# Forty-seven DMA issues moved from the sync engine's queue to GpSimd's in a hybrid attention and mLSTM step

## The chip, the cores and the metric

The kernel runs on one core of one Trainium2 chip. The metric is the device time of one execution in microseconds (us). The core has five engines that work side by side: TensorE (PE, matrix products), VectorE (DVE), ScalarE (ACT), GpSimd (POOL) and the sync engine (SP). Each works through its own list of instructions in order. DMAs are issued by an engine's queue: an issue waits in its place in that list until its semaphores allow it, and whatever stands behind it on the same engine waits too. Nearly all DMAs of this kernel are issued by SP, a few by ACT, and two by POOL.

## The reference, cut to what matters

One layer of a diffusion backbone on 128 context tokens and 1024 latent tokens (nine blocks of 128), with rows of 1024 numbers:

```python
h = rmsnorm(x, norm1_w) * (1 + sc1) + sh1
aq, ak, av, mq, mk, mv, mo, mg = jnp.split(h @ w_in, SPLIT_POINTS, axis=-1)
...
attn_o = attention(aq, keys, vals)          # 8 query heads, 2 key heads
...
hm = (hm.reshape(B, T, MLSTM_WIDTH) * jax.nn.sigmoid(mo.astype(F32))).astype(x.dtype)
mix = jnp.concatenate([attn_o, hm], axis=-1) @ w_out
x = x + g1 * mix
h2 = rmsnorm(x, norm2_w) * (1 + sc2) + sh2
x = x + g2 * swiglu(h2, w_gu, w_down)
```

`hm` is the result of a bidirectional mLSTM (a matrix memory, scanned in chunks of 128 tokens). The shifts, scales and the gates `g1` and `g2` come from the conditioning, one set for context tokens and one for latent tokens. The outputs are the normalised rows `y`, the new keys and values, and the mLSTM states.

## The kernel before, in words

The nine blocks of tokens are taken in three groups of three (block 0 holds the context tokens). The input projection and the mLSTM heads come first; beside the projections of the four heads the attention of the three groups is woven in (lines 1740 to 1748). Group 0 keeps its attention results in SBUF. The results of groups 1 and 2 are stored to DRAM, block by block, as `o_d` (line 1164); the last of group 2 are made while the FFN of group 0 already runs.

At the end of the mLSTM stage POOL makes the weighted values `wv` for the memory update (line 840), multiplies and normalises the results (lines 970 and 977) and the results go to DRAM as `hm_d` (line 982; for the last two blocks of the last head by POOL's own queue).

`prefill` (line 1258) then does the half of the output projection that reads the mLSTM results, block by block, and adds it to the rows with the gate `g1`. The rows of groups 0 and 1 stay in SBUF; those of group 2 (`c == 2`) are loaded, added to by POOL (line 1314) and stored to DRAM as `x1_d` (line 1315). They come back later through `new_x1(2)` (line 1183).

The FFN of group 0 follows in five groups of hidden features (`GROUPS`). `gate_up` (line 1477) loads two weight pieces for each block of 128 features, splits each on ACT and DVE into a high and a low half (`load_piece`, lines 173 to 178), and forms three products for one of full precision. POOL makes the low half of the hidden features (`hl`, line 1497). `down` (line 1500) loads the gate rows `gl` and `gx` for 512 columns (`gate_bc`, lines 1189 and 1193), one buffer each, loads the pieces of `w_down`, and adds each block's product to the rows (`add_gated`, lines 1204 and 1205 on DVE). Raw weights land in two buffers (`raw`); a buffer is free when DVE has made the low half from it (line 145).

Beside it, `attention_side` runs the rest of the attention and the attention half of the output projection for groups 1 and 2 (`attn_out`, line 1406): a pair of gate rows `hmr` (`row_pair`, line 1243), the stored results `o` (line 1416), their halves (line 1418), the products and the gated add. After that the rows are normalised (`stats`, `features6`, line 1554) and transposed by PE (line 124) into operands `Bt` (line 1569) for groups 1 and 2, whose FFN is done together by a seven-product scheme after Strassen (`pair6`, lines 1620 to 1622, and `down6`, lines 1688 to 1690) until the end. `gs6` (line 1853) is one more pair of gate rows.

What sets the order: `hot(n)` raises the priority of a block, `tc.issue_after` puts an instruction behind another one, and `weave` interleaves main and side work by hand. The order on each engine's list is otherwise chosen by a planner that works with estimated times (`TC_OPTS = dict(schedule_with_timeline_sim=True)`, line 1868), and all semaphores are set by it. `dma` is `nc.sync.dma_start` and `pool` is `nc.gpsimd` (lines 55 and 56).

## Time and profile before

| | |
|---|---|
| median of 3 runs | 1530.39 us (1525.09 to 1530.83) |
| the profiled execution | 1527.74 us, its span 1526.0 us |
| PE busy | 1427.3 us (94%) |
| DVE busy | 1129.1 us (74%) |
| ACT busy | 813.6 us (53%) |
| POOL busy | 218.4 us (14%) |
| granted PE clock, mean | 0.979 |
| SP's and ACT's DMA queues | 45.8% and 1.1% of the DMA engines' time |
| POOL's DMA queue | 0.1%, 0.39 MB |

A profile describes one execution. Busy time counts an engine's instructions, not its waits. A line of waits names the engine that waited, what it was about to do, and the instruction or DMA that came last before it could go on; then the total, the number of waits and the longest. A line of DMA issues gives the transfer, the queue (SPq, ACTq, POOLq), the number, the size and, where it can be told, the median time from issue to landing. A line of one source line gives the shortest, median and longest duration in ns. `L1189` is line 1189 of the kernel; lines of a helper such as `sub` (145) or `transpose` (124) stand for many callers, which the names of the tiles tell apart.

### The profile page before, as it was taken

How to read it: one execution, taken by the hardware profiler on the slowest of the kernel's cores; microseconds unless marked ns; L12 is line 12 of the kernel's file. 1: busy time of each engine (PE TensorE's matmuls, PEld its weight loads, DVE VectorE, ACT ScalarE, POOL GpSimd, SP SyncE). 2: the span in 40 equal slices, each digit the busy share in tenths (PEclk: the TensorE clock that was granted, in tenths of full speed). 3: DMA queues.
4: the chain of work that ended last, by engine and by line, in shares of the span. 5: the costliest groups of instructions: out<-in, count | busy, mean ns of one | idle time of the engine just before them, and what ended most of it. 6: DMA issues, size and time to landing. Idle time of an engine off the chain costs nothing. (4 is left out here: it accounts for less than half of the span.)

```text
span 1526.0 us, 22787 instructions
## 1 busy us (share of the span) xinstructions
PE 1427.3 (94%) x8282; PEld 1064.8 (70%) x8282; DVE 1129.1 (74%) x2280; ACT 813.6 (53%) x1525; POOL 218.4 (14%) x310
## 2 busy tenths in 40 slices
PE   6889999998899889999999988989999999999994
PEld 3635667766677667978998977966766667676763
DVE  4978556775867878658678766969877696986857
ACT  5855467956767546555675944735233150523233
POOL 0122423232224335210100100100000000000000
PEclk9999999999999899999999999999999999999997
DMA  9575224553668764768687745334122130412112
GB/s 374 155 222 180 79 70 76 127 109 59 103 146 174 180 207 112 202 173 216 177 194 175 172 128 159 104 117 166 56 83 84 41 125 1 139 49 76 35 35 83
DMA packets 254182, 197.02 MB, mean 129 GB/s; under 512 B 166830, under 2 KB 208006, under 8 KB 254070
## 3 DMA queue, kind: packets, MB, share of 16 engines
q1 hardware_dynamic: 251070, 189.56, 45.8%
q10 hardware_dynamic: 2872, 5.62, 1.1%
q8 instruction: 65, 1.06, 0.3%
q14 instruction: 47, 0.39, 0.1%
q0 software_dynamic: 128, 0.39, 0.1%
HBM read 143.94 MB, written 13.26 MB: 103 GB/s over the span
## 5 line engine op out<-in xcount | busy, mean ns | idle before, releaser
L1621 PE MATMUL mm<-Bt,A 128*128 128x384 f16 x616 | 200.8, 326 | 0.0
L1620 PE MATMUL mm<-Bt,A 128*128 128x384 f16 x616 | 199.4, 326 | 0.5 <-DVE c L1641 0.5
L1622 PE MATMUL mm<-Bt,A 128*128 128x384 f16 x616 | 197.5, 326 | 0.0
L174 ACT CAST whi<-raw 128x1024 fp32r<-128x1024 f32 (+1 forms) x102 | 103.0, 1013 | 134.2 <-DMA raw<-in_w_down_dram 43.9
L145 DVE TENSOR_TENSOR wlo<-raw,whi 128x1024 fp32r<-128x1024 f32 (+1 forms) x102 | 121.3, 1190 | 52.9 <-ACT whi L174 50.5
L1136 DVE SCALAR_TENSOR_TENSOR pl<-pr,st,ph 128x1152 f16<-128x1152 f32 (+1 forms) x72 | 95.2, 1322 | 40.8 <-ACT ph L1135 40.8
L1473 PE MATMUL mm<-aTh,whi 128*128 128x384 f32 x352 | 121.3, 345 | 2.4 <-DVE tn L1492 1.2
L1474 PE MATMUL mm<-aTl,whi 128*128 128x384 f32 x352 | 120.2, 342 | 0.0
L1475 PE MATMUL mm<-aTh,wlo 128*128 128x384 f32 x352 | 120.0, 341 | 0.0
L1132 ACT ACTIVATE pr<-S,st 128x1152 f32<-128x1152 f32 (+1 forms) x72 | 81.5, 1132 | 51.8 <-DVE st L1131 50.5
L1131 DVE TENSOR_REDUCE st<-S 128x1 f32<-128x1152 f32 (+1 forms) x72 | 88.9, 1234 | 21.5 <-PE S L1129 21.4
L526 PE MATMUL wi<-headw,hT 128*128 128x384 f16 x288 | 93.9, 326 | 1.2 <-ACT th L816 1.2
L527 PE MATMUL wi<-headw,hT 128*128 128x384 f16 x288 | 93.9, 326 | 0.0
L528 PE MATMUL wi<-headw,hT 128*128 128x384 f16 x288 | 93.9, 326 | 0.0
L1135 ACT ACTIVATE ph<-pr,st 128x1152 f16<-128x1152 f32 (+1 forms) x72 | 83.7, 1163 | 17.1 <-DVE st L1134 8.5
L1129 PE MATMUL S<-kst,qT 128*128 128x384 f32 (+1 forms) x400 | 86.7, 350 | 3.6 <-ACT pr L1132 3.6
L1620 PEld LDWEIGHTS <-A 128*128 128x128 f16 x616 | 60.2, 98 | 42.5 <-issue 3.5
L1622 PEld LDWEIGHTS <-A 128*128 128x128 f16 x616 | 60.3, 98 | 39.8
L1621 PEld LDWEIGHTS <-A 128*128 128x128 f16 x616 | 60.3, 98 | 39.6 <-issue 0.6
L1606 ACT ACTIVATE A<-S,six 128x1024 f16<-128x1024 f32 x44 | 49.9, 1145 | 71.0 <-PE mm L1622 54.0
L1204 DVE TENSOR_TENSOR t<-mm,hmr 128x512 f32<-128x512 f32 x84 | 54.3, 683 | 41.0 <-PE mm L1690 33.3
L145 POOL TENSOR_TENSOR hl<-tn,hl 128x384 fp32r<-128x384 f32 x22 | 29.8, 1355 | 335.5 <-ACT hl L1496 307.9
(460 smaller groups left out, 3737.8 us busy)
## 6 DMA issues: line engine op xcount, KB each, us to landing
raw<-in_w_gu_dram SPq DMA_DIRECT2D x88, 512.0 KB, 3.4
raw<-in_w_down_dram SPq DMA_DIRECT2D x40, 512.0 KB, 3.8
a<-in_w_ada_dram SPq DMA_DIRECT2D x24, 512.0 KB, 5.6
iraw<-in_w_in_dram SPq DMA_DIRECT2D x32, 256.0 KB, 3.4
x<-in_x_sample_dram SPq DMA_DIRECT2D x11, 512.0 KB, 6.0
raw<-in_w_out_dram SPq DMA_DIRECT2D x10, 512.0 KB
aw<-in_w_ada_dram SPq DMA_DIRECT2D x8, 512.0 KB, 5.3
aw<-in_w_ada_dram SPq DMA_DIRECT2D x16, 256.0 KB, 7.8
```

Of the source, the lines that this page charges most:

```text
L145: (dve if eng == "dve" else pool).tensor_tensor(out=out, in0=full, in1=hi, op=ALU.subtract)
L174: nc.scalar.copy(hi[:, :n], raw[:, :n])
L526: mm(ps[:, :n], ah, wh[:, k % 2, c0 : c0 + n], start=(k == 0), stop=False)
L527: mm(ps[:, :n], ah, wl[:, k % 2, c0 : c0 + n], start=False, stop=False)
L528: mm(ps[:, :n], al, wh[:, k % 2, c0 : c0 + n], start=False, stop=(k == KD - 1))
L1136: dve.scalar_tensor_tensor(out=plv, in0=prv, scalar=st[:, 3:4], in1=phv, op0=ALU.mult, op1=ALU.subtract)
L1473: mm(ps, wh[:, k, :], th[:, k, :], start=(k == 0), stop=False)
L1474: mm(ps, wh[:, k, :], tl[:, k, :], start=False, stop=False)
L1475: mm(ps, wl[:, k, :], th[:, k, :], start=False, stop=(k == KD - 1))
L1620: mm(ps, wh[:, k], bt[:, 0, k], start=first and k == 0, stop=False, skip_group_check=True)
L1621: mm(ps, wh[:, k], bt[:, 1, k], start=False, stop=False, skip_group_check=True)
L1622: mm(ps, wl[:, k], bt[:, 0, k], start=False, stop=k == 3, skip_group_check=True)
```

## The change

Each of these DMAs is issued by POOL instead of SP; nothing else differs in the program text. The issues are the stores of attention results of groups 1 and 2 (line 1164), the loads of group 2's rows (1183), the gate rows of the FFN of group 0 (1189 and 1193), the pairs of gate rows (1243), the stores of group 2's rows in `prefill` (1315), and the loads of the stored attention results (1416).

```diff
@@ attention
-                                dma(spill[i].rearrange("p (k x) -> p k x", k=4), oT[i])
+                                pool.dma_start(spill[i].rearrange("p (k x) -> p k x", k=4), oT[i])
@@ new_x1
-            dma(x1[i], x1_d[i])
+            pool.dma_start(x1[i], x1_d[i])
@@ gate_bc
-        dma(gl, g_d[idx, 1:2, cs].to_broadcast([P, 512]))
+        pool.dma_start(gl, g_d[idx, 1:2, cs].to_broadcast([P, 512]))
...
-        dma(gx, g_d[idx, 0:1, cs].to_broadcast([P, 512]))
+        pool.dma_start(gx, g_d[idx, 0:1, cs].to_broadcast([P, 512]))
@@ row_pair
-            dma(gl, row[n * 512 : (n + 1) * 512].rearrange("(o n) -> o n", o=1).to_broadcast([P, 512]))
+            pool.dma_start(gl, row[n * 512 : (n + 1) * 512].rearrange("(o n) -> o n", o=1).to_broadcast([P, 512]))
@@ prefill, half
-                dma(x1_d[i][:, cs], xt)
+                pool.dma_start(x1_d[i][:, cs], xt)
@@ attn_out
-                dma(o, spilled[i].rearrange("p (k x) -> p k x", k=4))
+                pool.dma_start(o, spilled[i].rearrange("p (k x) -> p k x", k=4))
```

## The prediction

> **What bounds the kernel now.** I read the page first, then busy time by stretches, the waits of TensorE (PE), the waits of the sync engine's queue (SPq), the list of DMA issues, and the timeline where PE stands still. The change touches only work between 422 us, where the first moved store begins to wait, and about 1010 us, where the last gate row is loaded (rows for both stand further down).

> ```profile
> span 1526.0 us, 22787 instructions
> ```
> ```profile
> core 0: us, PE busy (x) PEld busy (x) DVE busy (x) ACT busy (x) POOL busy (x), PEclk, DMA share, GB/s
> 420.00:592.00 172.00, 155.65 (x956) 119.01 (x954) 135.92 (x333) 109.41 (x258) 64.93 (x90) 0.96 0.71 172
> 500.00:592.00 92.00, 79.09 (x451) 60.26 (x450) 77.56 (x211) 51.37 (x112) 35.31 (x34) 0.94 0.67 183
> 592.00:1010.00 418.00, 399.79 (x2160) 359.15 (x2159) 299.10 (x459) 248.63 (x368) 50.31 (x37) 0.99 0.61 163
> 700.00:880.00 180.00, 180.00 (x1038) 165.62 (x1037) 136.43 (x195) 127.38 (x185) 13.81 (x11) 1.00 0.75 186
> ```

> From 592 to 1010 us PE is busy 399.79 of 418 us: 18.2 us are idle, which is all that a better queue could win there. From 700 to 880 us, where most of the moved gate rows fall, nothing is idle. The stretch with more idle time, 500 to 592 us (12.9 us), has one moved DMA issue near it (an attention store at 493 us) and none inside. So PE sets the end of this part, and the first question is whether the 18.2 us come from SP's queue. They are mostly two pauses:

> ```profile
> PE mm L124 <- ACT t L1554: 5.1, 1, 5.1
> PE mm L1215 <- ACT whi L174: 2.8, 1, 2.8
> ```
> ```profile
> 947.23 0.16 DVE L141 SCALAR_TENSOR_TENSOR ry<-rt,ry 128x3 f32<-128x3 f32 x1
> ```
> ```profile
> 949.43 1.88 PE L124 MATMUL mm<-ident,t 128*128 128x128 f32 x8 [5.14 <-ACT t L1554]
> ```

> The longest, 5.1 us, ends at 949.4 us with the transposes of the third group's normalised rows. ScalarE (ACT) makes those rows with the reciprocal root that VectorE (DVE) finishes only at 947.4 us (947.23 + 0.16). A weight that arrived earlier would not have ended this pause. Only the 2.8 us name a weight piece, and the remaining pauses are shorter. Now what SP's queue itself waits for from 592 to 1010 us:

> ```profile
> SPq L173 <- DVE wlo L145: 128.0, 48, 10.1
> ...
> SPq L1193 <- DVE t L1204: 14.4, 5, 5.8
> SPq L1164 <- DVE oS L1158: 11.0, 4, 6.1
> SPq L1189 <- DVE t L1204: 11.0, 6, 3.2
> ```

> The weight loads (line 173) wait 128 us in 48 waits for DVE to give back the raw buffer that they load into, as there are two. The moved DMAs (gate rows at lines 1189 and 1193, attention stores at 1164) hold the queue some 36 us. That looks like much, but a weight load that comes to the head of the queue earlier will in most cases stand there and wait for its buffer.

> **The change part by part.** The moved issues, with their number:

> ```profile
> gl<-g_d SPq DMA_DIRECT2D x12, 256.0 KB
> gx<-g_d SPq DMA_DIRECT2D x10, 256.0 KB, 3.9
> ...
> hm_d<-hm SPq DMA_DIRECT2D x10, 192.0 KB, 5.0
> ...
> o_d<-oS SPq DMA_DIRECT2D x6, 256.0 KB
> ...
> hmr<-g_d SPq DMA_DIRECT2D x6, 256.0 KB
> x_d<-t SPq DMA_DIRECT2D x6, 256.0 KB
> t<-o_d SPq DMA_DIRECT2D x6, 256.0 KB, 3.3
> x<-x_d SPq DMA_DIRECT2D x3, 512.0 KB, 4.3
> ...
> hm_d<-hm POOLq DMA_DIRECT2D x2, 192.0 KB, 2.3
> ```
> ```profile
> L1189 SPq DMA_DIRECT2D gl<-g_d x10: 319/327/835, 638.1 to 1008.3; - x10
> ```
> ```profile
> L982 POOL DMA_DIRECT2D hm_d<-hm x2: 584/650/715, 541.0 to 564.1; - x2
> ```

> Ten of the twelve gl loads move (line 1189; the two of line 1235 stay), with 10 gx, 6 o_d stores, 6 hmr, 6 x_d stores, 6 o_d loads and 3 x_d loads: 47 issues. Bytes and DMA engines stay as they are.

> What SP loses: 47 issues at the median 0.327 us of line 1189, 15.4 us, and the waits ahead of them. What that is worth to PE lies between 0 and all 18.2 idle us. I take 0, because the row nearest to it is the weight loads' 128 us of waiting for buffers, and because the longest pause ends with a DVE chain.

> What POOL gains: 47 issues at 0.65 us (the median of its two own DMAs), 30.6 us. POOL is idle 418 - 50.31 = 367.7 us from 592 to 1010 us, so as work it is hidden. As POOL works in order, each issue also waits there for what it waits for on SP, and what is queued behind it waits too. In the FFN part these are the low halves of the hidden features:

> ```profile
> L145 POOL TENSOR_TENSOR hl<-tn,hl x22: 1005/1023/3711, 648.4 to 1000.1; 128x384 fp32r<-128x384 f32 x22
> ```

> They are 22 in 352 us, and a gate row is waited for while a down projection ends, when the halves of the next group are still to come. So the cover is POOL's idle time, and I cost this at 0. If the cover were gone, one store or load could be held up as one of those halves was, 3.71 us instead of 1.02, that is by 2.7 us.

> The landing: POOL's two stores to hm_d took 2.3 us from issue to landing, SP's ten to the same tensor 5.0 us, SP's moved loads 3.3 to 4.3 us. For POOL's loads there is no row; they are bounded by -2.7 us (2.3 against 5.0) and +2.7 us (the held-up half). Nearest is the same kind of transfer on the same queue, which shows no penalty. Who waited for a landing of the moved ones from 592 to 1010 us:

> ```profile
> DVE t L1204 <- DMA gl<-g_d: 2.5, 2, 1.4
> ...
> ACT Bt L1569 <- DMA o_d<-oS: 1.7, 1, 1.7
> ```

> Of the ten gl loads two were waited for, at most 1.4 us each. One attention store holds back a Strassen operand on ACT by 1.7 us. For this one I take the longer issue, 0.65 - 0.33 = 0.3 us, as if it lay on the path, with -1.7 us (the wait gone) and +2.7 us as ends.

> [...]

> The sum: 0 (SP) + 0 (POOL) + 0.3 us (landing) on the profiled execution's 1527.74 us (span 1526.0 and 1.7 around it) is 1528.0 us. That execution lies 2.65 us under the median 1530.39 us of the three runs, so against the median the forecast is 1530.7 us: no change. A measurement of this kernel can tell about 0.5%, 7.7 us, from no change.

> **The rivals.** First, faster: SP's queue is what made the pauses, by delaying weights and transposes a little everywhere. For it speak the 36 us that the moved DMAs held the queue; against it that PE idles 0 us from 700 to 880 us, with the same gate rows in the queue. Taking half of the 18.2 us gives 1530.39 - 9.1 = 1521.3 us.

> Second, slower: POOL stands still ahead of a store with work behind it that PE needs. The place is the end of the mLSTM stage, where the first two attention stores lie and where POOL makes the weighted values (line 840) that PE multiplies:

> ```profile
> SPq L1164 <- DVE dn L964: 7.6, 1, 7.6
> SPq L1164 <- DVE oS L1158: 1.9, 1, 1.9
> ```
> ```profile
> 427.06 0.75 POOL L840 TENSOR_TENSOR wv<-va,QT 128x129 f32<-128x129 f32 x2 [1.29 <-ACT va L813]
> ```
> ```profile
> 430.20 0.32 SPq L1164 DMA_DIRECT2D o_d<-oS  x1
> ```

> SP stood 7.6 us until 430.2 us for the first store. Were it POOL that stood there, the products of 427.06 us would come after 430.2 + 0.65 us, 3.8 us late. With the second store's wait of 1.9 us and its 0.65 us of issue that is 6.4 us; with both waits whole and both issues stretched to 3.71 us it is 7.6 + 1.9 + 7.4 = 16.9 us. The middle is 11.6 us: 1542.0 us. It decides as soon as POOL is made to wait there longer than those products can be late, which is little. Against it: POOL's order is worked out anew, and the store may be put behind the products.

> Third, the planner: the order on every engine comes from estimated times (line 1868), and 47 issues on another queue change them. The new order may be better or worse, on PE too. The measure of what order can do is a stretch of the same kernel whose order fits badly: 12.9 us idle from 500 to 592 us. It gives 1517.5 us or 1543.3 us. Against it: the stretch from 700 to 880 us is filled by whatever order the weights allow.

> **How the numbers follow.** No change: 0.50. SP's queue gives back half the pauses: 0.12. POOL's wait in the mLSTM stage: 0.13. The planner's order better: 0.13, worse: 0.12. So faster by over 0.5%: 0.25, within 0.5%: 0.50, slower by over 0.5%: 0.25. Of the forecast's own case I hold 1523 to 1538 us. For 8 in 10 the range must take in most of the outer cases, of which the lowest stands at 1517.5 and the highest at 1543.3 us, with the bound of 16.9 us above (1547.3 us): 1515 to 1547 us.

> **What would show it.** Right: 47 more POOL issues of about 0.65 us; SP's waits on lines 1164, 1189 and 1193 gone and the weight loads' waits on DVE's low halves grown by about as much; PE idle from the end of the prefill to the last down projection still near 18 us. The first rival shows as PE idle there near 9 us; the second as a longer POOL wait ahead of line 1164 and PE waiting for line 840; the third as another order of lines on PE with idle time moved to other stages. I am wrong if POOL's issues take several us each and the low halves come late, so that PE waits at lines 1215 to 1217 for POOL.

## The result and the profile after

| | before | changed |
|---|---|---|
| median | 1527.74 us (4 runs, 1524.93 to 1530.83) | 1548.58 us (4 runs, 1545.03 to 1550.0) |
| ratio | | 1.0132, 95% interval 1.01 to 1.0165 |
| the profiled execution | 1527.74 us, span 1526.0 us | 1547.23 us, span 1545.1 us |

The change makes the kernel slower by about 20 us, 1.3%. The forecast was no change, 1530.7 us, and the result lies just above the range's end of 1547 us.

The page of the changed kernel begins so (busy time, share of the span, instructions):

```profile
span 1545.1 us, 22814 instructions
...
PE 1434.9 (93%) x8282; PEld 1070.0 (69%) x8282; DVE 1130.3 (73%) x2280; ACT 814.1 (53%) x1525; POOL 246.5 (16%) x357
```

The work on PE is the same 8282 matmuls. PE's idle time is 110.2 us (1545.1 - 1434.9) against 98.7 us before (1526.0 - 1427.3), so 11.5 of the 19.1 us of span are idle time. The other 7.6 us are busy time of the same matmuls. Part of it has nothing to do with the change: in the first 100 us, ahead of every moved transfer, the granted clock was 0.88 in this execution and 0.95 in the one before, and PE was busy 77.11 us against 75.11. That cost no time further on: the last low half of the prefill (`aTl`, line 145) begins at 606.26 us, and at 606.00 us before. How the rest divides was not measured. Stretches that hold pauses show a lower granted clock: 0.91 from 640 to 700 us (0.97 before), and 0.74 from 960 to 980 us, around the longest pause (0.91 around the same pause before, 940 to 960 us).

The stretches of the prediction, with the same columns (PE, weight loads, VectorE, ScalarE, GpSimd, granted clock, DMA share, GB/s):

```profile
420.00:592.00 172.00, 154.68 (x960) 118.10 (x959) 137.68 (x335) 109.26 (x257) 67.43 (x92) 0.97 0.71 173
...
592.00:1010.00 418.00, 390.22 (x2088) 350.47 (x2088) 291.52 (x447) 247.39 (x366) 74.41 (x79) 0.97 0.60 159
700.00:880.00 180.00, 176.95 (x993) 161.17 (x992) 135.39 (x197) 123.11 (x179) 23.31 (x28) 0.99 0.73 185
```

Up to 592 us nothing is lost: 960 matmuls in 154.68 us of busy time, against 956 in 155.65. From 592 to 1010 us PE's idle time grows from 18.2 to 27.8 us, and fewer matmuls are done in the same time (2088 against 2160). What PE waits for there, and what SP's queue waits for (total, number, longest):

```profile
PE mm L124 <- ACT t L1554: 7.1, 1, 7.1
PE mm L1473 <- ACT whi L174: 6.0, 1, 6.0
PE po L1154 <- DMA plT<-pl: 3.8, 3, 3.0
```
```profile
SPq L173 <- DVE wlo L145: 173.2, 56, 13.7
```

The second line of PE's waits is new: 6.0 us for a weight piece that ScalarE had not yet split. (The third, for a transpose that SP issues, is not followed here.) SP's queue has lost its waits for the moved transfers and waits 45 us longer for VectorE to give back raw buffers, 173.2 against 128.0. The waits of GpSimd ahead of its own transfers that no semaphore in the profile explains ("issue"), from 592 to 1040 us:

```profile
POOL x_d L1315 <- issue: 10.6, 5, 3.4
...
POOL gx L1193 <- issue: 9.3, 2, 6.6
...
POOL hmr L1243 <- issue: 5.3, 1, 5.3
POOL gl L1189 <- issue: 5.0, 2, 3.4
...
POOL x L1183 <- issue: 4.7, 1, 4.7
```

Together 34.9 us. They are not the instructions themselves, which take 0.55 us each. Here is GpSimd's timeline where the first time is lost (start, duration, what ran; in brackets its idle time just before, and what ended it), first in the kernel before, then in the changed kernel; then ScalarE's and PE's in the changed kernel:

```profile
634.45 1.29 POOL L1314 TENSOR_TENSOR t<-t,t 128x512 f32<-128x512 f32 x1 [1.20 <-DMA t<-in_x_sample_dram]
648.41 1.02 POOL L145 TENSOR_TENSOR hl<-tn,hl 128x384 fp32r<-128x384 f32 x1 [12.67 <-ACT hl L1496]
```
```profile
635.01 1.29 POOL L1314 TENSOR_TENSOR t<-t,t 128x512 f32<-128x512 f32 x1 [2.62 <-DMA t<-in_x_sample_dram]
637.90 0.57 POOL L1189 DMA_DIRECT2D gl<-g_d  x1 [1.60 <-issue]
641.84 0.55 POOL L1315 DMA_DIRECT2D x_d<-t  x1 [3.38 <-issue]
648.94 0.55 POOL L1193 DMA_DIRECT2D gx<-g_d  x1 [6.55 <-issue]
649.50 1.27 POOL L1314 TENSOR_TENSOR t<-t,t 128x512 f32<-128x512 f32 x1
...
656.42 1.62 POOL L145 TENSOR_TENSOR hl<-tn,hl 128x384 fp32r<-128x384 f32 x1 [3.02 <-ACT hl L1496]
```
```profile
648.79 1.06 ACT L178 ACTIVATE jk<-whi 128x1024 bf16<-128x1024 f32 x1 [7.13 <-DMA x_d<-t]
...
650.81 1.06 ACT L178 ACTIVATE jk<-whi 128x1024 bf16<-128x1024 f32 x1 [0.87 <-POOL t L1314]
```
```profile
646.61 0.34 PE L1475 MATMUL mm<-aTh,wlo 128*128 128x384 f32 x1
652.95 0.69 PE L1473 MATMUL mm<-aTh,whi 128*128 128x384 f32 x1 [6.00 <-ACT whi L174]
...
655.33 0.52 PE L1475 MATMUL mm<-aTh,wlo 128*128 128x384 f32 x1
```

Read it from the end. PE stands 6.00 us for a weight piece. ScalarE had stood 7.13 us until 648.79, because its scratch tile `jk` (line 178) shares its buffers with the rows `t` of line 1314, and the one it was to write was still being stored to `x_d`. That store was issued at 641.84, after 3.38 us of standing behind the gate row `gl`. ScalarE then waited once more for the last add of line 1314, and this add, which before the change began at 634.45 us, began at 649.50: it is behind the gate row `gx` on GpSimd's list, and `gx` stood 6.55 us until 648.94, 0.15 us after ScalarE saw the store land. The matmuls behind the pause take longer as well: one of line 1475 takes 0.34 us ahead of it and 0.52 us behind it, and from 651 to 658 us the granted clock is 0.52 (1.00 in the same stretch before).

What `gx` stood for is the landing of that store. The longest landing of a store of line 1315 was 6.8 us, and 641.84 + 6.8 = 648.6. This is no single case. The trace has the semaphore steps that tell of each landing. By them no transfer of GpSimd's in this kernel is issued earlier than 0.30 us after the one ahead of it has landed, and 28 of the 48 that follow another are issued 0.30 to 0.31 us after it, under whatever name the profile puts the wait. So in this kernel an issue on GpSimd's queue stands, and everything behind it in GpSimd's order with it, until the transfer issued before it has landed.

### The profile page after: what moved, and what is told of

Its sections match the earlier page's. It is cut to its first block, busy times and chain, and to the rows that moved or that the text cites. A ratio compares the mean times of both kernels' runs of the same rounds, so it can differ in the third digit from the quotient of the medians.

```text
span 1545.1 us, 22814 instructions
## 1 busy us (share of the span) xinstructions
PE 1434.9 (93%) x8282; PEld 1070.0 (69%) x8282; DVE 1130.3 (73%) x2280; ACT 814.1 (53%) x1525; POOL 246.5 (16%) x357
## 5 line engine op out<-in xcount | busy, mean ns | idle before, releaser
L174 ACT CAST whi<-raw 128x1024 fp32r<-128x1024 f32 (+1 forms) x102 | 102.9, 1012 | 133.1 <-DMA raw<-in_w_down_dram 43.2
L145 DVE TENSOR_TENSOR wlo<-raw,whi 128x1024 fp32r<-128x1024 f32 (+1 forms) x102 | 120.5, 1182 | 59.2 <-ACT whi L174 57.8
L1131 DVE TENSOR_REDUCE st<-S 128x1 f32<-128x1152 f32 (+1 forms) x72 | 88.9, 1235 | 28.2 <-PE S L1129 27.8
L1135 ACT ACTIVATE ph<-pr,st 128x1152 f16<-128x1152 f32 (+1 forms) x72 | 83.7, 1163 | 18.2 <-DVE st L1134 7.2
L1622 PEld LDWEIGHTS <-A 128*128 128x128 f16 x616 | 60.3, 98 | 39.8
L1621 PEld LDWEIGHTS <-A 128*128 128x128 f16 x616 | 60.3, 98 | 39.0
L1204 DVE TENSOR_TENSOR t<-mm,hmr 128x512 f32<-128x512 f32 x84 | 54.5, 684 | 41.4 <-PE mm L1690 32.3
L1688 PE MATMUL mm<-whi,hl 128*128 128x512 f32 x192 | 76.8, 400 | 0.0
## 6 DMA issues: line engine op xcount, KB each, us to landing
raw<-in_w_gu_dram SPq DMA_DIRECT2D x88, 512.0 KB, 4.1
raw<-in_w_down_dram SPq DMA_DIRECT2D x40, 512.0 KB, 4.0
a<-in_w_ada_dram SPq DMA_DIRECT2D x24, 512.0 KB, 6.9
iraw<-in_w_in_dram SPq DMA_DIRECT2D x32, 256.0 KB, 3.4
x<-in_x_sample_dram SPq DMA_DIRECT2D x11, 512.0 KB, 5.5
raw<-in_w_out_dram SPq DMA_DIRECT2D x10, 512.0 KB
aw<-in_w_ada_dram SPq DMA_DIRECT2D x8, 512.0 KB, 5.5
aw<-in_w_ada_dram SPq DMA_DIRECT2D x16, 256.0 KB, 8.3
```

The costliest lines, as they stand in the source:

```text
L145: (dve if eng == "dve" else pool).tensor_tensor(out=out, in0=full, in1=hi, op=ALU.subtract)
L174: nc.scalar.copy(hi[:, :n], raw[:, :n])
L1621: mm(ps, wh[:, k], bt[:, 1, k], start=False, stop=False, skip_group_check=True)
L1622: mm(ps, wl[:, k], bt[:, 0, k], start=False, stop=k == 3, skip_group_check=True)
L1688: mm(ps, hl[:, 0, sl], wh[:, k % 2, :], start=(k == 0), stop=False)
```

## The experiments

**Theory Q** says just that: GpSimd's queue holds one transfer at a time. **Theory O** (order) is the third rival of the prediction: the planner laid out the other engines' lists differently (VectorE's and ScalarE's from about 635 us on, PE's from 662 us), and the new order is slower. **Theory S** (semaphores) is GpSimd's waiting in order for the buffers that its loads fill, with nothing else.

The program is made with `dynamic_dma_scratch_size=256` in both kernels; here the size is called GpSimd's DMA scratch, in bytes. If that is the room for GpSimd's transfers, more of it lets more than one be under way. A larger scratch leaves all engines' lists of instructions as they are in the changed kernel, so it tells Q from both others.

```diff
-    nc = _bacc.Bacc("TRN2", target_bir_lowering=False, num_devices=1, dynamic_dma_scratch_size=256)
+    nc = _bacc.Bacc("TRN2", target_bir_lowering=False, num_devices=1, dynamic_dma_scratch_size=384)
```

> The changed kernel with GpSimd's DMA scratch at 384 bytes in place of 256; every engine's list of instructions stays the changed kernel's, in the same order. Theory Q (GpSimd's queue: a DMA issue stands on the engine until the DMA issued before it has drained, as in the changed trace's 6.55 us ahead of one gx load, and the adds behind it come late): with room for a second DMA most of the idle time put down to issue ahead of GpSimd's DMAs goes (10.6 us ahead of the x_d stores, 9.3 ahead of gx), and the time comes back to 1530 to 1538 us. Theory O (order: the planner lays out the lists of TensorE, VectorE and ScalarE in another order from about 660 us on, and that order is slower): nothing changes, 1545 to 1550 us. Theory S (semaphores: in-order waits of GpSimd for the buffers its loads fill, without any drain): nothing changes either, 1545 to 1550.

Measured: 1530.31 us, ratio to before 1.0014 (1.0 to 1.0028). Some 18 of the 20 us are back, with the same instructions in the same order on every engine. O and S fall as main causes. Three runs ask whether it is a matter of more room or of room for whole transfers, and whether the size does something by itself (the same line with 192 and 320 bytes in the changed kernel, and with 384 bytes in the kernel before).

> The changed kernel with 192 bytes of DMA scratch in place of 256, all lists of instructions the same. Theory Q in its step form (the queue has room for whole transfers: one at 256 bytes, two at 384): one at 192 too, so nothing changes against the changed kernel: 1545 to 1552 us. Theory Q in a graded form (less room, longer waits): slower still, 1555 to 1570.

> The changed kernel with 320 bytes of DMA scratch, all lists the same. Step form of theory Q: if two transfers fit in 320 bytes, the time is that of 384 bytes, 1528 to 1533 us; if they don't, that of 256, 1545 to 1550. Graded form: half way between, 1536 to 1542.

> The kernel before with 384 bytes of DMA scratch, lists the same. All theories: no change, 1526 to 1530 us, since only two transfers of it are GpSimd's and they lie in the mLSTM stage. Were it faster by 0.5% or more, the size itself and not GpSimd's transfers would be what the first experiment moved.

Measured: 192 bytes 1546.1 us, ratio 1.0114 (1.0079 to 1.0148); 320 bytes 1530.56 us, 1.0019 (1.0005 to 1.0033); the kernel before with 384 bytes 1526.11 us, 0.999 (0.9974 to 1.0006). It is one step: 192 and 256 bytes are slow, 320 and 384 are not, and in the kernel before the size does nothing. The graded form of Q falls. GpSimd's waits and timeline with 320 bytes, at the same place:

```profile
POOL x_d L1315 <- issue: 4.5, 2, 2.7
...
POOL gx L1193 <- issue: 1.6, 1, 1.6
```
```profile
630.49 0.57 POOL L1189 DMA_DIRECT2D gl<-g_d  x1
633.76 0.54 POOL L1315 DMA_DIRECT2D x_d<-t  x1 [2.71 <-issue]
634.39 0.55 POOL L1193 DMA_DIRECT2D gx<-g_d  x1
636.51 1.29 POOL L1314 TENSOR_TENSOR t<-t,t 128x512 f32<-128x512 f32 x1 [1.57 <-DMA t<-in_x_sample_dram]
638.21 0.56 POOL L1315 DMA_DIRECT2D x_d<-t  x1 [0.41 <-POOL t L1314]
...
647.56 1.64 POOL L145 TENSOR_TENSOR hl<-tn,hl 128x384 fp32r<-128x384 f32 x1 [8.80 <-ACT hl L1496]
```

A store and a gate row are issued 0.63 us apart; no store of line 1315 landed in less than 3.3 us here, so two transfers are under way at once. All along the list it is the same: 22 of the 48 issues that follow another come before the transfer ahead has landed (23 with 384 bytes), but none, with either size, earlier than 0.31 us after the landing of the one two places ahead. The last add begins 2.1 us after `gx` instead of standing behind 6.55 us. Since executions begin with small offsets, a distance inside each is compared: from the start of the last two low halves of the prefill (`aTl`, one row of the timeline) to the first of the FFN (`hl`) it is 43.7 us before, 51.4 us after, 45.9 us with 320 bytes. To the last of the FFN's 22 low halves it is 395.3, 413.5 and 399.2 us, so nearly the whole loss arises between these two, 7.7 of its 18.2 us at the place shown.

Why the step lies between 256 and 320 bytes, no run shows.

The second set asks which of the transfers matter. Only the named lines are GpSimd's, with 256 bytes of scratch.

```diff
 (only this line changed)
-                dma(x1_d[i][:, cs], xt)
+                pool.dma_start(x1_d[i][:, cs], xt)
```

> Only the six stores of x1_d are on GpSimd's queue; gate loads, attention results and third group's rows stay with SyncE. Theory Q: the stores stand behind one another only, 2.6 to 10 us apart, so little stands: 1528 to 1534 us, and ScalarE's weight split at 640 to 655 us is not held up. Theory O: the lists differ from the kernel before in some hundred places of TensorE, so a part of the loss may show, 1528 to 1540. Theory S: the store waits for the add ahead of it on the same engine, so nothing: 1528 to 1532.

Measured: 1528.13 us, 1.0002 (0.9986 to 1.0017). No cost.

```diff
 (the change, but with this line as before)
-                pool.dma_start(x1_d[i][:, cs], xt)
+                dma(x1_d[i][:, cs], xt)
```

> The change without the six stores of x1_d, which stay with SyncE. Theory Q: the first gate loads no longer stand behind a store, so the 8.8 us lost by 690 us fall to 0 to 4; the loads at 916 to 928 us still stand behind one another: 1535 to 1542 us. Theory O: TensorE's list differs from that before in about as many places as the changed kernel's, so 1540 to 1550. Theory S: gate loads wait for the tiles they fill as before, 1545 to 1550.

Measured: 1542.46 us, 1.0095 (1.0073 to 1.0118): half a microsecond above what Q gave. The distance to the first low half is 46.2 us, so most of the first loss is gone, as Q says.

```diff
 (only these two lines changed)
-        dma(gl, g_d[idx, 1:2, cs].to_broadcast([P, 512]))
+        pool.dma_start(gl, g_d[idx, 1:2, cs].to_broadcast([P, 512]))
...
-        dma(gx, g_d[idx, 0:1, cs].to_broadcast([P, 512]))
+        pool.dma_start(gx, g_d[idx, 0:1, cs].to_broadcast([P, 512]))
```

> Only the twenty loads of the gate rows gl and gx are on GpSimd's queue. Theory Q: a pair costs GpSimd about 3 us between its two halves, and ten pairs lie ahead of adds: part of the loss, 1532 to 1540 us. Theory O: lists in another order, 1535 to 1550. Theory S: GpSimd waits in these loads for VectorE's t at 18.9 and 23.9 us in all, whatever else is on its queue: most of the loss, 1538 to 1548.

Measured: 1528.73 us, 1.0004 (0.9992 to 1.0016). Here Q was wrong as I had put it, and S too: twenty transfers, nothing lost. Their waits put down to issue are 1.9 us in all. Here a pair that is only behind itself delays nothing that is needed. What costs should then be transfers of different parts that meet, so the next runs combine them.

```diff
 (lines 1189 and 1193 of the gate rows as above, and)
-                dma(x1_d[i][:, cs], xt)
+                pool.dma_start(x1_d[i][:, cs], xt)
```

> Gate rows and the six stores of x1_d on GpSimd's queue, 256 bytes of scratch; each part alone changed nothing (1528.7 and 1528.1 us). Theory Q: together they meet at 627 to 650 us, where a gate load stands between two stores ahead of the last two adds of L1314, so the changed kernel's first loss of some 8 us comes back, and only that: 1534 to 1538 us. Rival (each transfer on GpSimd's queue costs a fixed amount): 26 transfers that cost nothing in two parts cost nothing together, 1527 to 1530.

> The kernel of the run before with 320 bytes of scratch, all lists the same. Theory Q: the loss is gone, 1527 to 1531 us. Theory O: as the run before.

Measured: 1534.22 us, 1.0052 (1.0035 to 1.0069) with 256 bytes; 1527.6 us, 0.9995 (0.998 to 1.0011) with 320. Two parts that cost nothing alone cost 6.6 us together (by the medians), and nothing with room for two. GpSimd and ScalarE of the first of the two kernels, then GpSimd of the second:

```profile
638.41 0.55 POOL L1315 DMA_DIRECT2D x_d<-t  x1 [3.22 <-issue]
647.47 0.57 POOL L1193 DMA_DIRECT2D gx<-g_d  x1 [8.51 <-issue]
648.05 1.27 POOL L1314 TENSOR_TENSOR t<-t,t 128x512 f32<-128x512 f32 x1
```
```profile
647.27 1.06 ACT L178 ACTIVATE jk<-whi 128x1024 bf16<-128x1024 f32 x1 [11.68 <-DMA x_d<-t]
```
```profile
634.75 0.54 POOL L1315 DMA_DIRECT2D x_d<-t  x1 [1.47 <-issue]
636.85 0.57 POOL L1193 DMA_DIRECT2D gx<-g_d  x1 [1.56 <-DVE t L1313]
637.88 1.29 POOL L1314 TENSOR_TENSOR t<-t,t 128x512 f32<-128x512 f32 x1 [0.46 <-DMA t<-in_x_sample_dram]
```

It is the changed kernel's first loss by itself: `gx` stands until the store before it has landed, 8.51 us, with the add behind it and ScalarE's tile behind the store. With room for two, the same issue comes 2.1 us after the store's, while that store is under way (by the landings, it is the load `gl` two places ahead that it waits for, 0.31 us after whose landing it comes), and ScalarE does not wait for a store at all.

```diff
 (lines 1189 and 1193 of the gate rows as above, and)
-                                dma(spill[i].rearrange("p (k x) -> p k x", k=4), oT[i])
+                                pool.dma_start(spill[i].rearrange("p (k x) -> p k x", k=4), oT[i])
...
-                dma(o, spilled[i].rearrange("p (k x) -> p k x", k=4))
+                pool.dma_start(o, spilled[i].rearrange("p (k x) -> p k x", k=4))
```

> Gate rows and attention results (six stores, six loads) on GpSimd's queue; x1's stores and loads and the row of hmr stay with SyncE. Theory Q: the first loss (640 to 690 us) is gone, since no store of x1_d is ahead of the gate loads; the run of attention loads with gx among them, 12 us in the changed trace and 6 with the larger scratch, and the store of o_d with gl behind it remain: 1532 to 1539 us. Theory O: TensorE's list is another again, so 1535 to 1550. If it is no slower than gates alone (1528.7), the loss needs the loads of x1 or of hmr.

Measured: 1537.26 us, 1.0052 (1.0032 to 1.0071). And the attention results without the gate rows (the last two lines of that diff alone):

> Only the six stores and six loads of the attention results are on GpSimd's queue, 256 bytes of scratch. Theory Q: with no gate load between them the stores stand alone and only the three loads of one group follow each other, where no add waits behind: 1527 to 1531 us, so that the 9.8 us of gates and attention together come from their meeting. Rival (attention results alone carry the loss, by the later turn of o): 1534 to 1538.

Measured: 1527.13 us, 0.9991 (0.9969 to 1.0013). Again nothing alone, and 8 us together by the ratio, 10 by the medians. The first loss is absent from the pair (41.6 us to the first low half); it loses later. Part of that lies where the attention results of the last group are loaded: from the low half ahead of these loads to the next one it is 63.4 us, against 59.6 in the kernel before and 60.6 with the gate rows alone. The rest is not followed here. The same stretch in the changed kernel, and with 320 bytes:

```profile
915.14 1.32 POOL L145 TENSOR_TENSOR hl<-tn,hl 128x384 fp32r<-128x384 f32 x1 [9.15 <-issue]
916.40 0.56 POOL L1416 DMA_DIRECT2D t<-o_d  x1
920.55 0.55 POOL L1416 DMA_DIRECT2D t<-o_d  x1 [3.58 <-PE mm L1217]
923.80 0.55 POOL L1193 DMA_DIRECT2D gx<-g_d  x1 [2.71 <-issue]
927.88 0.54 POOL L1416 DMA_DIRECT2D t<-o_d  x1 [3.52 <-DVE t L1204]
...
980.78 1.58 POOL L145 TENSOR_TENSOR hl<-tn,hl 128x384 fp32r<-128x384 f32 x1 [21.05 <-ACT hl L1496]
```
```profile
904.30 1.31 POOL L145 TENSOR_TENSOR hl<-tn,hl 128x384 fp32r<-128x384 f32 x1 [7.94 <-issue]
905.55 1.09 POOL L1416 DMA_DIRECT2D t<-o_d  x2
910.53 0.54 POOL L1193 DMA_DIRECT2D gx<-g_d  x1 [3.89 <-DVE t L1204]
911.26 0.54 POOL L1416 DMA_DIRECT2D t<-o_d  x1 [0.19 <-issue]
...
964.55 1.58 POOL L145 TENSOR_TENSOR hl<-tn,hl 128x384 fp32r<-128x384 f32 x1 [20.52 <-ACT hl L1496]
```

The lists are the same. The third load comes 12.7 us after the low half in the changed kernel and 7.0 us after it with 320 bytes; the next low half 65.6 and 60.3 us after it. Two of the changed kernel's waits are put down to an engine here (`PE mm L1217`, `DVE t L1204`), but by the landings in the trace both issues come 0.30 to 0.31 us after the transfer ahead has landed. With room for two, the first two loads go out back to back and neither wait is there. So the name is only the last semaphore that came before the issue, and the waits named "issue" are not all of the standing.

```diff
 (the change, but with the gate rows as before)
-        pool.dma_start(gl, g_d[idx, 1:2, cs].to_broadcast([P, 512]))
+        dma(gl, g_d[idx, 1:2, cs].to_broadcast([P, 512]))
...
-        pool.dma_start(gx, g_d[idx, 0:1, cs].to_broadcast([P, 512]))
+        dma(gx, g_d[idx, 0:1, cs].to_broadcast([P, 512]))
```

> The change without the gate rows, which stay with SyncE: stores of o_d and x1_d, loads of x1, of the attention results and of hmr's row on GpSimd's queue. Theory Q: the transfers left meet each other less often, and no gate load is between two of them; the three loads of an attention result still come one behind another: 1528 to 1534 us. Rival (a fixed cost for each transfer, 20 us over 47): 27 of them, 1539 us.

Measured: 1533.15 us, 1.0035 (1.0017 to 1.0052), where a fixed price for each transfer asked for 1539. Here an attention load that stands for the one before it has a low half directly behind it:

```profile
662.48 0.54 POOL L1416 DMA_DIRECT2D t<-o_d  x1 [4.14 <-issue]
663.04 1.01 POOL L145 TENSOR_TENSOR hl<-tn,hl 128x384 fp32r<-128x384 f32 x1
```

This wait is not shown to be the cost: the kernel with the attention results alone has the same one (4.24 us ahead of the load at 659.92 us, the low half at 660.49 us) and is no slower. From 592 to 700 us PE pauses 7.2 us here, 4.1 us there and 3.4 us in the kernel before, and 1.8 us of the 7.2 are waits of lines 1473 and 1475 for weight pieces, which neither of the other two has. Which meeting of transfers makes them is not followed.

All kernels beside each other; the third column sums GpSimd's waits put down to issue ahead of the moved transfers, 592 to 1040 us, as in the five lines above:

| on GpSimd's queue | scratch, bytes | issue waits, us | ratio to before |
|---|---|---|---|
| all 47 | 256 | 34.9 | 1.0132 |
| all 47 | 192 | 49.4 | 1.0114 |
| all 47 | 320 | 6.7 | 1.0019 |
| all 47 | 384 | 8.5 | 1.0014 |
| all but x1's stores, 41 | 256 | 32.2 | 1.0095 |
| gate rows and attention results, 32 | 256 | 15.1 | 1.0052 |
| gate rows and x1's stores, 26 | 256 | 18.6 | 1.0052 |
| gate rows and x1's stores, 26 | 320 | 1.5 | 0.9995 |
| all but gate rows, 27 | 256 | 18.2 | 1.0035 |
| attention results, 12 | 256 | 6.2 | 0.9991 |
| x1's stores, 6 | 256 | 3.8 | 1.0002 |
| gate rows, 20 | 256 | 1.9 | 1.0004 |

The waits sort the kernels: under 9 us costs nothing or nearly so, 15 us and more costs 0.35% and up. They are no price list (192 bytes has more waits than 256 and no more time), since it matters what stands behind them. No kernel here is faster than the one before by more than its interval.

Open: with room for two the full change is still slower by 0.05 to 0.33%, 0.8 to 5.0 us, with 320 bytes, and by 0 to 0.28% with 384. Whether that is the changed order, GpSimd's waits in order or the 6.7 us of waits that are left, no run tells apart. In the kernel with room for two it is also the most that theories O and S can be worth together.

## Why the prediction was wrong

**The bound and SP's side were right.** PE sets the end of this part, and a freed SP queue is worth nothing to it: the waits for raw buffers took the time up, as the prediction said. With 320 bytes, where most of the loss is gone, they are 163.3 us against 128.0, that is 35.3 us more where the moved transfers had held the queue 36.4 us; the changed kernel's 173.2 us hold some of its loss as well. Two readings were off without bearing on the sum: the two pauses called most of the 18.2 us make 7.9 us of it, and 10 of the 20 gate rows, not most, were loaded from 700 to 880 us.

**The step that failed** is GpSimd's gain: "So the cover is POOL's idle time, and I cost this at 0", with 2.7 us as the most that one transfer could hold up. The work was sized rightly. GpSimd's busy time grew by 28.1 us (246.5 - 218.4) against 30.6 forecast, and it was hidden. The wait was not. The prediction let each issue wait "for what it waits for on SP"; here it also waits for the transfer before it to land, up to 6.55 us in the changed kernel and 8.51 us in the kernel with gate rows and x1's stores. GpSimd's idle time is cover only if nothing that PE needs stands behind the waiting issue. An add of line 1314, and through its buffers ScalarE's weight splits, stood behind it, and so did low halves of hidden features. The sum with 0 at this place would have needed about 18 us, which is what room for two transfers gives back (1548.58 to 1530.56 us).

The two GpSimd stores in the profile before could not show this: they lie 23 us apart (541.0 and 564.1 us) and landed in 2.3 us. The row that could have warned was the landing time of the moved transfers, 3.3 to 4.3 us at the median. With 0.55 us to issue, transfers that come closer than that are either under way together or one after the other, and the prediction never asked which.

**The landing** of 0.3 us was small, as forecast: on GpSimd's queue the loads took 3.6 to 4.5 us, on SP's 3.3 to 4.3, and ScalarE's wait for an attention store went from 1.7 to 2.4 us, 0.7 us more where the sum has 0.3. What the landing did was to hold GpSimd: VectorE's longest wait for a `gl` load, 6.04 us against 1.4 before, is for one that GpSimd issued at 841.51 us, 0.30 us after the store ahead of it had landed.

**The issues** of each moved line took 0.54 to 0.60 us on average, with VectorE 73% busy; the prediction had 0.65 us.

**The second rival** (slower: GpSimd stands still with work behind it that PE needs) had the mechanism nearly and the place wrong. At the end of the mLSTM stage the planner put the store behind the products, as the prediction's own objection said, and PE lost nothing:

```profile
427.90 0.75 POOL L840 TENSOR_TENSOR wv<-va,QT 128x129 f32<-128x129 f32 x2 [1.29 <-ACT va L813]
...
431.33 0.72 POOL L1164 DMA_DIRECT2D o_d<-oS  x1 [1.69 <-DVE dn L964]
```

Its 1542.0 us came from other waits than those that cost the 20 us, and its bound of 1547.3 us was passed. **The third rival**, the planner's order, did happen, and is worth at most 5 us as far as the kernel with room for two shows it. **The first**, a faster kernel, found nothing for it.

Of the signs named beforehand, 47 issues of 0.55 us and SP's waits came as forecast. "PE idle still near 18 us" did not (27.8). The sign of being wrong was half right: low halves came late, but it was the gaps ahead of the issues that took several microseconds, not the issues, and the new wait of PE names ScalarE's weight split, not GpSimd.

## What to carry to other kernels

Before moving transfers to GpSimd's queue, lay their issue times beside their landing times: where two come closer than one landing, ask how many the queue holds, and what GpSimd has to do behind them. Here GpSimd's idle time hid 28.1 us of added work, and not the waits of its issues, such as the 6.55 us ahead of one `gx`. Try the parts alone and in pairs, since here each of the three tried alone was free; and if the parts must share the queue, room for a second transfer was worth 18 us.
